# Attention scores of two heads at once, on the upper and lower 64 rows of the array

## Chip, cores and metric

The kernel runs on one core of a Trainium2 chip. The metric is device time in microseconds (us) from start to end of one execution; three runs of the kernel before gave 984.19, 984.31 and 984.76 us, median 984.31 us. The core has five engines that run their own instruction lists in order and meet at semaphores: TensorE (PE, matrix products; PEld is its loading of weights), VectorE (DVE), ScalarE (ACT), GpSimd (POOL) and SyncE (SP), on which this kernel issues all its transfers (DMA).

## The reference, cut to what matters

One decoder layer over 1024 tokens of width 1024: a projection, an attention branch (8 heads), a gated linear branch, their merge, and a gated embedding. The change is in the attention branch:

```python
def mla_attention(q_nope, q_rope, k_nope, k_rope, v):   # 8 heads, 64 + 32 wide; k_rope is shared by all heads
    ...
        sc = (jnp.einsum('bqhd,bkhd->bhqk', qn_i, k_nope).astype(jnp.float32)
              + jnp.einsum('bqhr,bkr->bhqk', qr_i, k_rope).astype(jnp.float32)) * scale
        mask = kpos[None, :] <= qpos[:, None]
        sc = jnp.where(mask[None, None], sc, -jnp.inf)
        pr = jax.nn.softmax(sc, axis=-1).astype(v.dtype)
        return jnp.einsum('bhqk,bkhd->bqhd', pr, v)
```

## The kernel before, in words

**Precision.** Inputs are float32. A factor is split into a rounded high part and the low rest (`split`: ScalarE copies into the rounded type, VectorE subtracts), and a product is the sum of three: high by high, high by low, low by high (`mm3`, lines 145 to 147). A group of such products into one PSUM bank is a `bank`.

**Stages.** First the projections of x and the gated linear branch (0 to some 470 us), then attention (some 548 to 760 us), then the merge, the output product and the gated embedding. Products that have no hurry are interleaved as filler by generators (`stream`, `embed`): in attention these are `yb` (branch output of the linear part, `d<-oh,wh`), later `emb` (`e<-wh,wh`) and the first of `ya` (the attention branch's own output product).

**Attention.** The queries' 32 rope rows of all heads are made in `rope_queries`, four heads at a time, and written to scratch memory (`d_rq`). `make_pair` makes the tiles of two heads: of each head `qh`, `ql`, `kh`, `kl` (high and low part of queries and keys), 96 rows of one tile for the even head (64 plain and 32 rope rows) and 128 for the odd head (its plain rows in the lower half of the tile, its rope rows in the upper half twice, with the key's halved to make up). The product of both heads lands in one bank, so the even head's 64 rows are copied to their own tile by a DMA within SBUF (L864), and rope rows come by DMA from `d_rq` and `krt` (L845, L849, L867, L871). `scores` goes by one head and half of the queries: for each block of 128 queries, over at most 512 keys at a time (a chunk), three products over 96 or 128 rows into a bank `s`; VectorE takes it out with scale, mask and running minimum (L914), ScalarE takes the exponential (L924). `weighted` transposes these rows (`pt`, L963), splits them, and multiplies by the values (`o`, L954 and L955). The loop at the end of the stage interleaves the scores of one head with `weighted` of the one before it, `make_pair` of the next pair, and filler.

**Products over 64 rows elsewhere.** The linear branch has products that use half of the array's rows: L379 (`z`, two rounded products of 512 columns, between full ones) and in `gla` L559, L619, L628 and L690. These float32 products appear as two records each in the trace. In `cross` (L559) the two heads, on rows 0 to 63 and 64 to 127, alternate. At L628 the loop over the two heads is the outer one, so that the eight products of one head stand ahead of the eight of the other:

```python
for hd in range(2):
    for c in range(4):
        for j in (0, 64):
            ...
            nc.tensor.matmul(L[j : j + 32, o0 + 32 : o0 + 64], r32[rows(hd), i0 : i0 + 32], ...)   # shortened
```

**What sets the order.** The order in which code is written is a wish; a scheduler in the compiler sets the order on each engine when the program is built, from its own estimate of times and from when buffers come free. [...] Buffers are `NSLOT` + `NMORE` slots of 4 KB per partition, and the PSUM banks: in attention four `d`, three `s`, one `o`.

## Time and profile before

| | |
|---|---|
| runs | 984.19, 984.31, 984.76 us |
| profiled execution | 983.49 us, span of its instructions 981.7 us |
| TensorE busy | 955.8 us, 97% |
| VectorE, ScalarE, GpSimd busy | 590.2, 413.1, 128.1 us |
| mean granted clock of TensorE | 0.99 |

The span runs from the first to the last instruction; the execution's own time is 1.8 us longer, and 0.8 us below the median of the runs. [...]

### The profile page before, as it was taken

Reading aid. Unit: us, or ns where it says so; the run is one execution under the profiler, and the core shown is the slowest. Engines: PE = TensorE matmul, PEld = TensorE weight load, DVE = VectorE, ACT = ScalarE, POOL = GpSimd, SP = SyncE. Lnnn points to the kernel's source line nnn. Section 1 sums busy time; section 2 is a strip of 40 time slices with the busy share of each in tenths; the row PEclk is TensorE's granted clock in tenths of the full one; section 3 lists DMA queues with packets and bytes.
Section 4 is the critical chain, followed back from the end, with each engine's and each line's share of the span. In section 5 each row is a group of like instructions: output and inputs, shape, how many; then the busy total and the mean of one; then the engine's idle time right before and its main releaser. Section 6 shows DMA issues by size and latency. Waiting matters only on the chain.

```text
span 981.7 us, 14101 instructions
## 1 busy us (share of the span) xinstructions
PE 955.8 (97%) x5216; PEld 794.3 (81%) x5216; DVE 590.2 (60%) x1227; ACT 413.1 (42%) x800; POOL 128.1 (13%) x103
## 2 busy tenths in 40 slices
PE   7999999999999999999999999997999999999995
PEld 5887877887887887888888778886888788889985
DVE  6737765574474474433476469785757863239666
ACT  7306731331331342321333257676885432228333
POOL 2100000000000000001101012235363000000422
PEclk9999999999999999999999999997999999999998
DMA  7200211122222122211253844537146761136112
GB/s 281 94 22 22 65 43 43 57 84 86 76 108 86 63 79 86 97 65 43 82 181 127 230 121 121 133 98 177 49 147 229 254 208 65 49 119 188 53 69 103
DMA packets 47828, 105.70 MB, mean 108 GB/s; under 512 B 6736, under 2 KB 9616, under 8 KB 47760
## 3 DMA queue, kind: packets, MB, share of 16 engines
q1 hardware_dynamic: 47760, 104.81, 33.1%
q8 instruction: 41, 0.67, 0.3%
q14 instruction: 27, 0.22, 0.1%
HBM read 72.18 MB, written 25.20 MB: 99 GB/s over the span
## 4 chain that ended last, share of the span: by engine, by line
PE 86%; DVE 6%; ACT 3%; DMA 3%; issue 2%; SPq 0%; DVEq 0%; ACTq 0%
PE d L145 19%; PE d L147 18%; PE d L146 18%; PE pt L963 3%; PE pg L147 3%; PE pg L146 3%; PE pg L145 3%; PE L L559 2%; PE o L955 2%; PE s L146 2%; PE o L954 2%; PE s L147 2%; PE s L145 2%; PE o L690 1%; DMA kl<-kl 1%
## 5 line engine op out<-in xcount | busy, mean ns | idle before, releaser
L145 PE MATMUL d<-xh,wh 128*128 128x512 f32 x544 | 215.9, 400 | 2.8 <-ACT xh L132 2.6
L146 PE MATMUL d<-xl,wh 128*128 128x512 f32 x544 | 214.5, 395 | 0.1
L147 PE MATMUL d<-xh,wl 128*128 128x512 f32 x544 | 213.3, 393 | 0.1
L145 PEld LDWEIGHTS d<-xh,wh 128*128 128x128 f32 x544 | 103.0, 190 | 28.1 <-ACT xh L132 4.6
L127 ACT ACTIVATE wh<-wr 128x1024 fp32r<-128x1024 f32 (+4 forms) x81 | 76.2, 943 | 114.3 <-DMA wr<-in_w_in 40.4
L146 PEld LDWEIGHTS d<-xl,wh 128*128 128x128 f32 x544 | 103.0, 189 | 21.9 <-DVE xl L133 0.8
L147 PEld LDWEIGHTS d<-xh,wl 128*128 128x128 f32 x544 | 102.7, 189 | 21.9 <-DVE wl L128 0.5
L128 DVE TENSOR_TENSOR wl<-wr,wh 128x1024 fp32r<-128x1024 f32 (+2 forms) x59 | 74.6, 1267 | 71.2 <-ACT wh L127 71.1
L145 PE MATMUL pg<-wh,gh 128*128 128x256 f32 (+1 forms) x200 | 62.7, 314 | 0.0
L146 PE MATMUL pg<-wl,gh 128*128 128x256 f32 (+1 forms) x200 | 62.5, 313 | 0.0
L147 PE MATMUL pg<-wh,gl 128*128 128x256 f32 (+1 forms) x200 | 62.5, 313 | 0.0
L128 DVE TENSOR_TENSOR pt<-pt,pt 128x512 fp32r<-128x512 f32 (+1 forms) x96 | 51.4, 550 | 17.1 <-ACT pt L127 16.9
L494 ACT ACTIVATE z<-z 128x512 f32<-128x512 f32 x32 | 20.2, 631 | 98.0 <-DVE z L466 94.2
L924 ACT ACTIVATE p<-p,nm 128x128 f32<-128x128 f32 (+3 forms) x64 | 49.3, 772 | 21.2 <-DVE nm L914 21.1
L466 DVE TENSOR_TENSOR z<-d,rb 128x512 f32<-128x512 f32 x32 | 22.1, 690 | 51.3 <-PE d L147 51.3
L127 ACT ACTIVATE pt<-pt 128x512 fp32r<-128x512 f32 (+1 forms) x96 | 44.6, 485 | 15.5 <-PE pt L963 13.6
L145 PE MATMUL d<-mh,wh 128*128 128x512 f32 x128 | 50.7, 399 | 0.0
L146 PE MATMUL d<-ol,wh 128*128 128x512 f32 x128 | 50.1, 392 | 0.4 <-DVE ol L128 0.4
L147 PE MATMUL d<-mh,wl 128*128 128x512 f32 x128 | 50.2, 392 | 0.0
L147 PE MATMUL d<-oh,wh 128*128 128x512 f32 x128 | 50.1, 391 | 0.0
L146 PE MATMUL d<-ml,wh 128*128 128x512 f32 x128 | 49.9, 390 | 0.0
L145 PE MATMUL d<-oh,wh 128*128 128x512 f32 x128 | 49.9, 395 | 0.0
(263 smaller groups left out, 1924.4 us busy)
## 6 DMA issues: line engine op xcount, KB each, us to landing
wr<-in_w_in SPq DMA_DIRECT2D x33, 512.0 KB
d_ta<-z SPq DMA_DIRECT2D x16, 256.0 KB
d_tb<-z SPq DMA_DIRECT2D x16, 256.0 KB
tb<-d_tb SPq DMA_DIRECT2D x16, 256.0 KB
d_zb<-tb SPq DMA_DIRECT2D x16, 256.0 KB
d_e<-er SPq DMA_DIRECT2D x16, 256.0 KB
ta<-d_ta SPq DMA_DIRECT2D x16, 256.0 KB
zb<-d_zb SPq DMA_DIRECT2D x16, 256.0 KB
```

The lines of the kernel that those rows point to most:

```text
L127: nc.scalar.activation(dst_hi, src, AF.Copy)
L128: (eng or nc.vector).tensor_tensor(dst_lo, src, f(dst_hi), op=ALU.subtract)
L145: nc.tensor.matmul(ps, lh, rh, start=first, stop=False)
L146: nc.tensor.matmul(ps, lh, rl, start=False, stop=False)
L147: nc.tensor.matmul(ps, ll, rh, start=False, stop=last)
L466: nc.vector.tensor_tensor(z, ps, rb[:, hs(h)], op=ALU.mult)
L494: nc.scalar.activation(z, z, AF.Tanh, scale=0.5)
L559: nc.tensor.matmul(L[:, hd * HALF + c * P : hd * HALF + (c + 1) * P], lt[rows(hd), cs], rt[rows(hd), cs], start=True, stop=True,)
L924: nc.scalar.activation(pt[:, :w], pt[:, :w], AF.Exp, bias=nm, scale=-1.0, accum_out=den)
L954: nc.tensor.matmul(po[:, n0:], vv, ts_[:, n0:HALF], start=kb == 0, stop=False)
L955: nc.tensor.matmul(po[:, n0:], vv, ts_[:, HALF + n0 : S], start=False, stop=kb == nk - 1)
L963: nc.tensor.transpose(pt[:, j * P : (j + 1) * P], pq[j][:, kb * P : (kb + 1) * P], ident)
```

## The change

Both heads of a pair now share tiles: rows 0 to 63 are the even head's, rows 64 to 127 the odd head's, as the product of `make_pair` leaves them in its bank. The rope part is a product of its own. For each chunk a head has five products over 64 rows: `kh,qh`, `kl,qh`, `kh,ql`, and with the rope rows `krt,rh` and `krt,rl`, where `krt` holds high and low part of the shared rope key (32 + 32 rows, and the same again for the lower half), and `rh`, `rl` hold a head's rope queries twice. Each head has its own bank, and the two heads' products are written in turn. `scores` goes by a pair. Both calls of `rope_queries` now stand ahead of the scores, its stores are of two halves, `make_pair` loads `rh` and `rl` by eight DMAs and copies nothing within SBUF. Banks are three `d` and four `s`; there are three more slots, for which the room comes from a smaller `dynamic_dma_scratch_size` (no DMA of this kernel is issued by GpSimd).

```diff
-NMORE = 4
+NMORE = 7
...
-                nc.scalar.activation(krt[64:96], f(krt[0:32]), AF.Copy, scale=0.5)
-                nc.scalar.activation(krt[96:128], f(krt[32:64]), AF.Copy, scale=0.5)
+                nc.scalar.activation(krt[64:128], f(krt[0:64]), AF.Copy)
...
-            get = psum_pool({"d": (HALF, 4), "S": (HALF, 3), "o": (HALF, 1)}, psB)
+            get = psum_pool({"d": (HALF, 3), "S": (HALF, 4), "o": (HALF, 1)}, psB)
...
-                for nm in ("qh", "ql", "kh", "kl"):
-                    for hn in (2 * pr, 2 * pr + 1):
-                        qk[nm, hn] = alloc(F32R, nm)
...
+                for nm in ("qh", "ql", "kh", "kl", "rh", "rl"):
+                    qk[nm, pr] = alloc(F32R, nm)
+                for y, nm in enumerate(("rh", "rl")):
+                    for i in range(4):
+                        r = 32 * (2 * pr % 4 + i // 2)
+                        nc.sync.dma_start(f(qk[nm, pr][32 * i : 32 * i + 32]), d_rq[pr // 2][y][r : r + 32])
...
-                    for y in range(2):
-                        nm = x + "hl"[y]
-                        t0, t1 = f(qk[nm, 2 * pr]), f(qk[nm, 2 * pr + 1])
-                        nc.sync.dma_start(t0[0:64], t1[0:64])
...
-                        mm3(st, qh_[:, qs], ql_[:, qs], kh_[:, c], kl_[:, c], True, True)
...
+                rows = (slice(0, 64), slice(64, 128))
+                q_, k_ = ([qk[n, pr] for n in ns] for ns in (("qh", "qh", "ql", "rh", "rl"), ("kh", "kl", "kh")))
+                k_ += [krt, krt]
...
+                        st = [get("S", "s")[:, :cw] for _ in range(2)]
+                        for i in range(5):
+                            for y, r in enumerate(rows):
+                                nc.tensor.matmul(st[y], q_[i][r, qs], k_[i][r, c], start=i == 0, stop=i == 4)
...
-    nc = bacc.Bacc("TRN2", target_bir_lowering=False, num_devices=1)
+    nc = bacc.Bacc("TRN2", target_bir_lowering=False, num_devices=1, dynamic_dma_scratch_size=1024)
```

The evictions and exponentials are the same in number and size, two heads after each other; the loop around them goes by pair and half, with `weighted` of two heads interleaved.

TensorE before, within the scores of an early head (`s` with its number is one bank; every product reads tiles of 96 or 128 rows, so all of this engine's work there uses the whole array):

```order
L145 MATMUL s_4309<-kh_4161,qh_4157 128x512
L146 MATMUL s_4309<-kl_4163,qh_4157 128x512
L147 MATMUL s_4309<-kh_4161,ql_4159 128x512
L145 MATMUL s_4345<-kh_4161,qh_4157 128x512
L146 MATMUL s_4345<-kl_4163,qh_4157 128x512
L147 MATMUL s_4345<-kh_4161,ql_4159 128x512
```

The two banks are of one head, 512 keys each; its other chunks follow in the same way.

TensorE now, early in the scores (`s_4384` is the even head's bank, `s_4385` the odd head's):

```order
L907 MATMUL s_4384<-kh_4215,qh_4213 128x512
L907 MATMUL s_4385<-kh_4215,qh_4213 128x512
L907 MATMUL s_4384<-kl_4216,qh_4213 128x512
L907 MATMUL s_4385<-kl_4216,qh_4213 128x512
L907 MATMUL s_4384<-kh_4215,ql_4214 128x512
L907 MATMUL s_4385<-kh_4215,ql_4214 128x512
L907 MATMUL s_4384<-krt_620,rh_4217 128x512
L907 MATMUL s_4385<-krt_620,rh_4217 128x512
L907 MATMUL s_4384<-krt_620,rl_4218 128x512
L907 MATMUL s_4385<-krt_620,rl_4218 128x512
L145 MATMUL d_4411<-oh_3282,wh_4329 128x512
```

Here the two heads' products alternate as they are written, and a product over the whole array follows. TensorE now, in the last pair (`s_6345` is the even head's bank, `s_6346` the odd head's; `o` and `pt` use the whole array):

```order
L907 MATMUL s_6345<-krt_620,rh_5701 128x256
L907 MATMUL s_6345<-krt_620,rl_5702 128x256
L954 MATMUL o_6071<-pt_6129,vp 128x512
L953 MATMUL o_6071<-pt_6139,vp 128x512
L962 MATMUL pt_6181<-ident,p_5617 128x128
L962 MATMUL pt_6181<-ident,p_5618 128x128
L954 MATMUL o_6071<-pt_6139,vp 128x512
L962 MATMUL pt_6189<-ident,p_5618 128x128
L953 MATMUL o_6071<-pt_6148,vp 128x384
L907 MATMUL s_6346<-kh_5699,qh_5697 128x256
L907 MATMUL s_6346<-kl_5700,qh_5697 128x256
```

The scheduler has put the five products of one head together and whole-array products between the two heads. Over the stage the 480 products over 64 rows stand in 64 runs, with whole-array instructions between them.

SyncE before, where the tiles of the last pair are filled:

```order
L864 DMA qh_5663<-qh_5664 64x1024
L864 DMA ql_5665<-ql_5666 64x1024
L871 DMA qh_5664<-d_rq_125 16x1024 x4
L871 DMA ql_5666<-d_rq_126 16x1024 x2
L137 DMA wr_5924<-in_pT 128x1024
L871 DMA ql_5666<-d_rq_126 16x1024
L864 DMA kh_5667<-kh_5668 64x1024
L943 DMA d_rc_117<-rr_5831 4x128
L864 DMA kl_5669<-kl_5670 64x1024
```

SyncE now, where the last pair's tiles are filled:

```order
L847 DMA rh_5701<-d_rq_125 32x1024 x2
L942 DMA d_rc_115<-rr_5657 4x128
L137 DMA wr_6008<-in_w_ple 128x1024
L847 DMA rh_5701<-d_rq_125 32x1024 x2
L945 DMA rB_5661<-d_rc_115 64x512
L944 DMA gt_5775<-d_gm_89 64x512
L847 DMA rl_5702<-d_rq_126 32x1024 x4
```

The copies of `qh`, `ql`, `kh` and `kl` within SBUF are gone; the loads of `rh` and `rl` read scratch that was written at the start of the stage. Outside the attention stage and the transfers that prepare it, TensorE's order is the same in both programs (up to its row 1983 of some 4500). On SyncE, ScalarE and VectorE one weight tile of a later product is now loaded and split near the start.

## Rows read from the trace of the kernel before

**Rows 1.** Windows; columns: stretch, length, busy time and count by engine, clock, DMA.

```profile
548.00:600.00 52.00, 49.34 (x272) 41.26 (x272) 35.89 (x103) 28.62 (x68) 8.95 (x7) 1.00 0.57 159
600.00:650.00 50.00, 48.83 (x294) 42.41 (x294) 42.26 (x119) 35.78 (x84) 12.84 (x10) 1.00 0.38 100
650.00:700.00 50.00, 43.81 (x232) 37.73 (x231) 32.77 (x88) 33.22 (x71) 20.22 (x12) 0.86 0.48 131
```

**Rows 2.** Waits of TensorE, 500 to 765 us: total, times, longest.

```profile
PE s L145 <- DVE pt L128: 5.5, 1, 5.5
PE s L146 <- DMA kl<-kl: 1.5, 2, 0.8
PE s L145 <- issue: 0.9, 1, 0.9
PE s L146 <- DMA ql<-d_rq: 0.8, 1, 0.8
```

**Rows 3.** Chain that ended last: start, duration, what.

```profile
673.15 5.92 DMA kl<-kl
```

**Rows 4.** Timeline of TensorE after the wait: start, duration, instruction.

```profile
678.01 0.44 PE L145 MATMUL s<-kh,qh 96*128 96x128 f32 x1 [5.53 <-DVE pt L128]
...
683.34 0.63 PE L147 MATMUL s<-kh,ql 96*128 96x512 f32 x1
683.76 0.63 PE L145 MATMUL s<-kh,qh 96*128 96x512 f32 x1
```

**Rows 5.** Windows around that wait.

```profile
676.00:680.00 4.00, 1.33 (x4) 1.17 (x5) 1.29 (x4) 2.51 (x5) 2.35 (x1) 0.50 0.98 240
...
684.00:688.00 4.00, 4.00 (x18) 3.71 (x18) 2.67 (x11) 2.83 (x10) 2.60 (x2) 0.50 0.32 132
```

**Rows 6.** Timeline of TensorE, score products of 128, 512 and 256 columns.

```profile
553.26 0.27 PE L146 MATMUL s<-kl,qh 96*128 96x128 f32 x1
...
553.37 0.28 PE L147 MATMUL s<-kh,ql 96*128 96x128 f32 x1
...
553.77 0.40 PE L146 MATMUL s<-kl,qh 96*128 96x512 f32 x1
...
554.00 0.40 PE L147 MATMUL s<-kh,ql 96*128 96x512 f32 x1
...
554.35 0.28 PE L146 MATMUL s<-kl,qh 96*128 96x256 f32 x1
...
554.47 0.28 PE L147 MATMUL s<-kh,ql 96*128 96x256 f32 x1
```

**Rows 7.** Groups of TensorE by form, 500 to 765 us: one score product.

```profile
L145 PE MATMUL s<-kh,qh 96*128 96x512 f32 x24 | 10.7, 446 | 0.0
```

**Rows 8.** Timeline of TensorE, two products over 64 rows between products over 128.

```profile
69.61 0.39 PE L147 MATMUL d<-xh,wl 128*128 128x512 f32 x1
69.93 0.73 PE L379 MATMUL z<-glow,wg 64*128 64x512 f32 x2
70.59 0.50 PE L145 MATMUL gv<-wh,xh 128*128 128x512 f32 x1
70.93 0.40 PE L146 MATMUL gv<-wl,xh 128*128 128x512 f32 x1
```

**Rows 9.** Timeline of TensorE, L559: products over 64 rows, two heads in turn.

```profile
128.74 0.39 PE L147 MATMUL d<-xh,wl 128*128 128x512 f32 x1
129.06 1.16 PE L559 MATMUL L<-r 64*128 64x128 f32 x16
130.15 0.50 PE L145 MATMUL d<-xh,wh 128*128 128x512 f32 x1
```

**Rows 10.** Timeline of TensorE, L222: products over all 128 rows.

```profile
459.37 1.84 PE L222 MATMUL ss<-ones,latents 128*128 128x1 f32 x16
```

**Rows 11.** Windows of L628 alone; count is of records running in the stretch.

```profile
142.09:142.25 0.16, 0.15 (x10) 0.16 (x11) 1.00 0.00 0
142.25:142.35 0.10, 0.10 (x22) 0.10 (x20) 1.00 0.00 0
```

## The prediction

> **What bounds the kernel now.** I read the page's busy shares first: TensorE is busy 97% of the span, no other engine above 60%. Most of the program is the same before and after, so I looked only at the attention stage, in windows [rows 1]: TensorE is busy 49.3 of 52, 48.8 of 50 and 43.8 of 50 us, VectorE at most 42.3 of 50. The reader should see that TensorE bounds the stage, with VectorE not far behind, and that the idle time of TensorE there is 2.7 + 1.2 + 6.2 = 10.1 us. The list of waits says what ends that idle time [rows 2]: 5.5 + 1.5 + 0.9 + 0.8 = 8.7 us stand before score products. The 5.5 us are put down to a VectorE instruction, but the chain shows a copy of `kl` within SBUF that lands after 5.92 us just then [rows 3], so the last pair's tiles were late. After that wait the products of 512 columns stand 0.42 us apart (683.34 to 683.76) [rows 4] and the granted clock is 0.50 until some time before 692 [rows 5]; the usual distance is 0.23 us [rows 6]. [...]

> **The products before.** The distance from start to start is the price: 0.11 us for 128 columns, 0.23 for 512, 0.12 for 256 [rows 6]; for 384 I estimate 0.17, which is 0.23 times 384/512. A head has twelve chunks: six of 512, two of 384, two of 256, two of 128 columns (a group of 24 for four heads gives the six [rows 7]). That is 6 x 0.23 + 2 x 0.17 + 2 x 0.12 + 2 x 0.11 = 2.18 us for one product each, and with three products and eight heads 52.3 us.

> **The products now.** A pair has five products per chunk and head, each over half of the rows. If both heads always ran beside each other, they would cost 5 x 4 x 2.18 = 43.6 us; if never, 10 x 4 x 2.18 = 87.2 us. Whether they do can be read from the linear branch. The 16 records of L559, two heads in turn, take 130.15 - 129.06 = 1.09 us with the change of mode below in it [rows 9]; 16 records over all rows, L222, take (1.84 - 0.25) / 15 = 0.106 us each, 1.7 us in all, though they have a single column [rows 10]. So halves of the array do work at the same time, at least in this form. The order of the changed kernel often puts the five products of one head ahead of the five of the other, so it matters whether the second head may start early. L628 has its heads in that order. In its first 0.16 us ten of its records start; in the next 0.10 us 22 are running, of which ten are those, so twelve new ones started in less time [rows 11]. The second head's sixteen therefore began while some of the first head's had not. I take each half as a queue of its own: a run of products costs the longer half's sum. Over the 64 runs in the new order, 23 hold products of one head only and cost 14.8 us, 41 hold both and cost 40.0 us; together 54.8 us, 2.5 us more than before. What the layout could win (8.7 us) the scheduler's grouping takes back.

> **The edges of the runs.** A run over 64 rows stands between products over 128 rows. The row to read is `z`, rounded products over 64 rows with 512 columns, as the new ones are [rows 8]: from the full product before them at 69.61 to the second full product after them at 70.93 there are 1.32 us. Four distances of 0.23 would be 0.92. The other 0.40 us are lost in four places of about 0.1: 0.32 instead of 0.23 from 69.61 to 69.93, another 0.1 within the two `z`, 0.1 before 70.59 and 0.34 instead of 0.23 after it. L559 has the same first step (128.74 to 129.06) [rows 9]. The score products over 96 rows show none of it: they follow each other at their usual distance [rows 6]. [...] At 64 runs the edges cost 64 x 0.40 = 25.6 us. They lie on TensorE, which bounds the stage; nothing hides them unless TensorE waits anyway. Bounds: `z` and L559 both also wait on semaphores at their start, so the edges might cost nothing where no wait stands; the upper bound is the 0.40 of each run.

> **What goes.** No copy within SBUF is left: the pair's product is split into its tile, and `rh` and `rl` come from scratch written long before. The waits on `kl`, `ql` and the first tiles go: -8.7 us. With them goes the stretch at half clock, 678.0 [rows 4] to about 688.1: 10.1 us x (1 - 0.23/0.42) = -4.6 us. What is late next are evictions: VectorE's work is the same, 42 of 50 us in the densest window [rows 1]; there are three `d` banks instead of four for the transposes; and the four `s` banks are only two chunks, since a chunk needs two. For new waits I take +2 us, between 0 and the 8.7 that go, nearer to 0 because a TensorE that has 28 us more work gives the others time to get ahead.

> **What costs nothing.** The two small copies of `krt` become one (ScalarE, 41% busy over the span). `rope_queries` for both groups stands ahead of the scores: the same 18 products, moved. Their eight stores become sixteen, on SyncE, with 36 filler and 30 projection products behind the last of them (66 x 0.23 = 15 us), as against a copy of 5.92 us as the longest seen [rows 3]; if one is later than that, the first `krt,rh` product waits and this falls into the +2. SyncE has 48 fewer transfers. The weight tile loaded early costs a copy each on ScalarE and VectorE at the start, where TensorE has other products to do; I price it at 0, at most 1 us either way.

> **Sum.** +2.5 + 25.6 - 8.7 - 4.6 + 2 = +16.8 us. The profiled execution took 983.5 us, so 1000.3; the runs' median is 0.8 above it, so 1001 us. With the edges at half price it would be 988, and with the larger new waits 1008: the likeliest case's own range is 988 to 1009.

> **Rivals.**
> - *The edges are free (faster).* If TensorE changes between halves and the whole array without loss when no wait stands there, the 25.6 us vanish and the removed waits decide: 1001 - 25.6 = 975 us. For it: each row that shows the loss also has a semaphore wait at its start, and the linear branch's runs are float32, except `z`. Against it: the same 0.09 to 0.11 us in each of the four places, at `z` as at L559, although the waits are on different engines. It decides from the point where a run's edges cost less than (16.8 / 64 =) 0.14 rather than 0.40 us.
> - *Strict order of starts.* If a product never starts before the one ahead of it in the program, the grouped products overlap only where the heads change. Counting the order so, the runs cost 64.6 us instead of 54.8: 1011 us. L628 [rows 11] speaks against it; but it has products of 32 columns, and a queue deep enough for these may not take five of 512 with their weights. [...]
> - *The heads don't run side by side at 512 columns.* No row shows two rounded products of this length in both halves. If they share a path that limits them, the products cost 87.2 us: 1001 + 32.4 = 1033 us. L559 and L628 speak against it, with shorter products.
> - *The tiles stay late.* If `rh` and `rl` wait for slots and land late, the 8.7 and 4.6 us stay: 1014 us. For it: six tiles per pair instead of eight, but two heads' rows `p` at once. Against it: three more slots, and the source is ready early.

> **Chances.** Likeliest case 0.55, free edges 0.19, strict order 0.10, no overlap 0.06, late tiles 0.06, and 0.04 that gains and losses meet within 0.2%, which is about what a measurement of this kernel can tell from no change (2 us). Faster gets nearly all of the free edges, 0.18; same 0.05; slower 0.77. The range reaches from the free edges' 975 to above the late tiles' 1014, 974 to 1016; outside are the case without overlap and the better half of the free edges, together a little under 0.2.

> **What would show it.** In the profile after, score products as 64*128, with a first product of a run about 0.32 us after a full one and 0.34 after the first full one behind it; the sum of score products and edges near 80 us instead of 52; no wait on `kl` and no window at half clock in the stage; the stage some 17 us longer, the stages around it unchanged. Two heads' products that start a few ns apart, also where the order has five of one head first, would show the queues right; 0.23 us between the heads would show strict order. I am wrong if a full product follows a half one after its usual 0.23 us.

## The result, and the profile after

The changed kernel takes 1027.87 us (median of four runs, 1027.56 to 1030.5) against 984.25 (four runs, 982.82 to 984.76): ratio 1.0451, 95% interval 1.0431 to 1.0472. The forecast was 1001 us, 974 to 1016. It is slower, as forecast, but by 43.6 us and not by 16.8. The profiled execution took 1027.97 us, its span is 1026.2; TensorE is busy 989.7 us of it, 96%.

The windows of the attention stage, in the columns of [rows 1]:

```profile
548.00:600.00 52.00, 40.70 (x224) 30.33 (x224) 24.04 (x67) 15.80 (x40) 3.85 (x3) 0.84 0.46 155
600.00:650.00 50.00, 49.31 (x285) 36.51 (x283) 34.48 (x99) 30.02 (x66) 7.73 (x6) 1.00 0.19 54
650.00:700.00 50.00, 48.83 (x290) 36.36 (x289) 34.11 (x92) 31.83 (x70) 12.65 (x9) 1.00 0.23 67
700.00:750.00 50.00, 48.87 (x283) 34.74 (x281) 33.04 (x92) 37.53 (x85) 22.23 (x14) 1.00 0.23 75
```

The hole of before, 43.8 of 50 us at clock 0.86 in the third window, is gone. A new one stands at the start of the stage: 40.7 of 52 us at 0.84. VectorE's densest window has 34.5 of 50 us, before 42.3. The waits of TensorE from 500 to 810 us, against [rows 2]:

```profile
PE s L907 <- DVE ql L128: 11.8, 1, 11.8
PE d L145 <- ACT wh L127: 2.8, 2, 2.2
PE d L145 <- ACT oh L127: 1.6, 1, 1.6
```

Before score products a single wait is left, and none is put down to a copy, as forecast; but that one, of the first score product of all, is 11.8 us. The chain of waits ahead of it, taken from the stretch 515 to 570 us (start, duration, what; [rows 3] was the like):

```profile
529.93 1.74 POOL rt L824
531.69 0.64 ACT rh L127
...
534.10 8.79 DMA d_rq<-rl
542.95 0.30 SPq L847
543.29 0.52 SPq L830
543.86 6.28 DMA d_rq<-rh
550.20 6.21 DMA tb<-d_tb
556.50 1.25 DVE tb L778 x2
...
558.43 1.26 DVE ql L128 x2
559.74 2.67 PE s L907 x15
```

Two stores of the queries' rope to scratch (L830) take 8.79 and 6.28 us from issue to landing, with other stores still on their way before them. SyncE's list has them one behind the other, and in its timeline they start so: the load of `rl` (542.95) reads what the first of them writes and starts when that has landed (534.10 + 8.79 = 542.89); the next stores of the second group start behind that load (543.29), and the loads of `tb` (for the filler) behind these (550.20). The loads of `tb` also need a temporary tile. `rt`, `rh`, `rl` and `tb` share six of them (`t2`), and before loads of `tb` SyncE waits 1.8 and 2.0 us more for the landings of two stores from these tiles. VectorE waits 8.9 us for the first `tb`, works on it and two more from 556.50, and starts the split of `ql`, which the first score product needs, only behind that (558.40). So that split, which reads nothing of what is stored, is held by two engines' queues and by the temporary tiles. The clock around it (windows; [rows 5]):

```profile
555.00:559.00 4.00, 0.00 (x0) 0.00 (x0) 2.50 (x5) 0.00 (x0) 0.00 (x0) 0.50 0.54 197
559.00:563.00 4.00, 3.71 (x22) 3.13 (x23) 3.42 (x12) 0.88 (x4) 0.00 (x0) 0.50 0.58 202
563.00:567.00 4.00, 4.00 (x12) 3.09 (x11) 0.33 (x2) 1.10 (x4) 0.00 (x0) 0.53 0.86 295
567.00:571.00 4.00, 4.00 (x23) 3.00 (x22) 1.73 (x5) 1.31 (x4) 0.00 (x0) 1.00 0.20 73
```

The stretch at half clock has moved with the wait: after it TensorE works for some 7 us at a granted clock of 0.50, its products of 512 columns 0.42 us apart (563.36 to 563.78). A second, short one (785.2 to 788.6) follows the wait of 2.2 us on `wh`:

```profile
785.00:789.00 4.00, 4.00 (x14) 3.24 (x13) 4.00 (x10) 2.44 (x5) 2.57 (x2) 0.57 0.70 198
```

Now the products themselves, TensorE's timeline where nothing waits ([rows 6, 8]; x2 are the two heads):

```profile
575.35 0.39 PE L147 MATMUL d<-oh,wh 128*128 128x512 f32 x1
575.67 0.50 PE L907 MATMUL s<-kh,qh 64*128 64x512 f32 x2
576.00 0.40 PE L907 MATMUL s<-kl,qh 64*128 64x512 f32 x2
576.24 0.40 PE L907 MATMUL s<-kh,ql 64*128 64x512 f32 x2
576.47 0.40 PE L907 MATMUL s<-krt,rh 64*128 64x512 f32 x2
```

Both heads go in one distance: 576.00 to 576.47 is 0.235 us for a pair, the 0.23 of one full product before. The first step costs 0.32 instead of 0.23, as at `z`, and the second 0.33, and the view shows no idle time there. Where the order has five products of one head first ([rows 11] was the like):

```profile
578.50 0.49 PE L907 MATMUL s<-kh,qh 64*128 64x512 f32 x1
578.83 0.39 PE L907 MATMUL s<-kl,qh 64*128 64x512 f32 x1
578.84 0.50 PE L907 MATMUL s<-kh,qh 64*128 64x512 f32 x1
579.06 0.39 PE L907 MATMUL s<-kh,ql 64*128 64x512 f32 x1
579.18 0.40 PE L907 MATMUL s<-kl,qh 64*128 64x512 f32 x1
```

The order has all five of the first head before the second's. The second's `kh,qh` starts at 578.84, ahead of the first's third, fourth and fifth. From there both halves run beside each other. So in these rows TensorE ran its list in order within each half alone.

Where TensorE's time went. I summed its records of the stage, each from its start to the next one's start, since their durations overlap (0.40 us at a distance of 0.235 above), idle time apart (before 470 to 765 us, after 470 to 810):

| us | before | after | difference | forecast |
|---|---|---|---|---|
| score products `s` | 59.0 | 70.7 | +11.7 | |
| `o` | 38.9 | 45.7 | +6.8 | |
| `pt` | 26.6 | 34.4 | +7.8 | |
| these three: products and edges | 124.5 | 150.7 | +26.3 | +28.1 |
| idle | 10.0 | 19.7 | +9.7 | -6.7 |
| filler and projections `d<-oh`, `d<-ol` (290 and 296 products) | 67.3 | 74.0 | +6.8 | |
| half clock, within the rows above (estimate) | 4.3 | 4.9 | +0.6 | -4.6 |

The edges also fall on what stands next to a run (behind `z` the first full product costs 0.34 us instead of 0.23 [rows 8]), so `o` and `pt` grow too. The last row is TensorE's time at clock 0.5 (9.4 us before, 10.8 after) times the prediction's 1 - 0.23/0.42. Before, it lies in `s`, `o` and `pt` almost alone (9.2 us); after, 3.8 us lie there and 7.1 in `d`. So at full clock the three would differ by an estimated 26.3 + 4.2 - 1.7 = +28.8 us. Of the +6.8 of `d`, six products more in the stretch are 1.4 and the half clock 3.2. The differences +26.3, +9.7 and +6.8 make 42.8 of the span's 44.5 us.

### The profile page after: what moved, and what is told of

It is laid out like the page before. It is cut to its first block, busy times and chain, and to the rows that moved or that the text cites. A ratio compares the mean times of both kernels' runs of the same rounds, so it can differ in the third digit from the quotient of the medians.

```text
span 1026.2 us, 14397 instructions
## 1 busy us (share of the span) xinstructions
PE 989.7 (96%) x5408; PEld 797.5 (78%) x5408; DVE 592.1 (58%) x1227; ACT 414.3 (40%) x799; POOL 131.3 (13%) x103
## 3 DMA queue, kind: packets, MB, share of 16 engines
q1 hardware_dynamic: 45264, 98.51, 28.8%
## 4 chain that ended last, share of the span: by engine, by line
PE 84%; DMA 7%; DVE 4%; ACT 1%; issue 1%; POOL 1%; SPq 1%; DVEq 0%; ACTq 0%; POOLq 0%
PE d L145 17%; PE d L147 17%; PE d L146 17%; PE s L907 7%; PE pg L147 3%; PE pg L146 3%; PE pg L145 3%; PE pt L962 3%; PE L L558 2%; PE o L954 2%; PE o L953 2%; DMA tb<-d_tb 1%; PE gv L146 1%; PE gv L145 1%; PE gv L147 1%
## 5 line engine op out<-in xcount | busy, mean ns | idle before, releaser
L128 DVE TENSOR_TENSOR wl<-wr,wh 128x1024 fp32r<-128x1024 f32 (+2 forms) x59 | 72.5, 1231 | 69.9 <-ACT wh L127 69.8
L923 ACT ACTIVATE p<-p,nm 128x128 f32<-128x128 f32 (+7 forms) x64 | 49.4, 772 | 45.9 <-DVE nm L910 45.5
L145 PE MATMUL d<-oh,wh 128*128 128x512 f32 x128 | 52.1, 411 | 4.3 <-ACT wh L127 2.2
L127 ACT ACTIVATE pt<-pt 128x512 fp32r<-128x512 f32 (+1 forms) x96 | 44.4, 484 | 25.4 <-PE pt L962 24.8
L147 PE MATMUL d<-oh,wh 128*128 128x512 f32 x128 | 51.9, 405 | 0.2 <-DVE wh L128 0.2
L465 DVE TENSOR_TENSOR z<-d,rb 128x512 f32<-128x512 f32 x32 | 22.1, 690 | 49.3 <-PE d L147 49.3
```

Of the source, the lines that this page charges most:

```text
L127: nc.scalar.activation(dst_hi, src, AF.Copy)
L128: (eng or nc.vector).tensor_tensor(dst_lo, src, f(dst_hi), op=ALU.subtract)
L145: nc.tensor.matmul(ps, lh, rh, start=first, stop=False)
L147: nc.tensor.matmul(ps, ll, rh, start=False, stop=last)
L465: nc.vector.tensor_tensor(z, ps, rb[:, hs(h)], op=ALU.mult)
L923: nc.scalar.activation(pt, pt, AF.Exp, bias=nm[y], scale=-1.0, accum_out=den4[y][:, qb - 4 * hf : qb - 4 * hf + 1])
```

## Experiments

Ratios are to the kernel before on the same chip (in brackets the 95% interval); 1% is 9.8 us. Five of them (3, 4, 5, 7 and 13) leave work out, as their expectations say. Idle times of TensorE are from 470 to 810 us of each span (before: 10.4, the change: 19.7).

| kernel | median us | ratio |
|---|---|---|
| changed kernel | 1027.87 | 1.0451 (1.0431 to 1.0472) |
| 1 rope stored whole | 1020.30 | 1.0331 (1.0282 to 1.0380) |
| 2 products of a chunk held together | 1128.01 | 1.1449 (1.1372 to 1.1525) |
| 3 pairs, whole array | 1012.60 | 1.0250 (1.0176 to 1.0324) |
| 4 before, middle product over 64 rows | 1024.83 | 1.0374 (1.0295 to 1.0453) |
| 5 as 3, four `d` banks | 992.87 | 1.0069 (1.0049 to 1.0089) |
| 6 as 1, late rope | 1025.58 | 1.0384 (1.0355 to 1.0413) |
| 7 before, no copies | 975.37 | 0.9875 (0.9847 to 0.9902) |
| 8 as 1, heads in turn | 1017.32 | 1.0303 (1.0269 to 1.0337) |
| 9 as 1, four `d` banks | 1020.24 | 1.0351 (1.0327 to 1.0375) |
| 10 before, three `d` banks | 1009.24 | 1.0234 (1.0199 to 1.0268) |
| 11 before, copies earlier | 987.28 | 1.0019 (0.9996 to 1.0042) |
| 12 before, rope first | 992.13 | 1.0080 (1.0052 to 1.0107) |
| 13 as 5, late rope | 984.27 | 0.9983 (0.9960 to 1.0006) |
| 14 as 9, late rope | 1021.83 | 1.0366 (1.0335 to 1.0397) |

**1. Rope stored whole.** The changed kernel with the stores of before.

```diff
-d_ = d_rq[g][y].rearrange("(h s r) c -> s h r c", s=2, h=4)
-for s_ in range(2):
-    nc.sync.dma_start(d_[s_][:, :, hs(h)], f(r_[64 * s_ : 64 * s_ + 64]))
+nc.sync.dma_start(d_rq[g][y][:, hs(h)], f(r_))      # and rh, rl read back 16 rows at a time
```

> The changed kernel with one edit: the rope queries are stored as in the kernel before (one transfer of 128 rows per part and half instead of two of 4 x 16 rows), and read back by 16 rows. Theory: the new transfers of 4 x 16 rows land late (6 to 9 us in the chain), hold SyncE's list and the temporary buffers, and so cause the wait of 11.8 us ahead of the first score product and some 3.7 us at half clock behind it; without them 1028 - 15 = about 1012 us. Rival: the start of the stage is late because both rope groups stand ahead of the scores and because of three d banks, whatever the form of the store; then the wait stays and the time is 1024 to 1028 us.

1.2% less than the change, in the middle between the two. The edit also reads `rh` and `rl` back in 64 loads instead of 32. The wait before the first score product, and a store in the chain:

```profile
PE s L906 <- DVE ql L128: 2.8, 2, 2.6
```

```profile
531.80 2.18 DMA d_rq<-rh
```

2.18 us for a whole tile of 256 KB, where halves of 128 KB took 6.28 and 8.79; the longest wait falls from 11.8 to 2.6 us, so most of it came from the form of the store. With the stores under way, the busy share of the 16 DMA engines (the last column but one) was 0.26 in the change, as much as 4.2 engines busy throughout, and 0.98 in 1; what in the pattern makes the difference is not shown:

```profile
534.00:539.80 5.80, 5.80 (x27) 4.80 (x26) 1.75 (x3) 0.00 (x0) 1.19 (x1) 1.00 0.26 97
```

```profile
532.80:534.00 1.20, 1.20 (x7) 1.00 (x6) 1.17 (x3) 0.00 (x0) 0.00 (x0) 1.00 0.98 362
```

Some 33 us over the kernel before remain.

**2. A chunk's ten products held together** (the kernel of 1, with a critical section around them).

```diff
+with tc.tile_critical():
     for i in range(5): ...
```

> The kernel of e1_store_whole, and the ten score products of a chunk kept together and in their written order (48 runs over 64 rows instead of 65; by halves as queues the products cost 43.6 us instead of 55.3). Theory: each run costs about 0.4 us at its edges, so 17 x 0.4 + 11.7 = 18 us less than e1, about 993 us. Rival: ten products that need two free banks at once make TensorE wait for evictions, which takes the gain back: within 5 us of e1.

It failed as an experiment: the section also stops what stands around it, TensorE is idle 75.5 us, much of the stage runs at half clock (its mean from 500 to 750 us is 0.84), and the two longest of many waits are these:

```profile
PE s L907 <- ACT p L923: 16.6, 12, 2.3
PE s L907 <- issue: 9.1, 9, 3.6
```

**3. Whole array** (the kernel of 1, three products a head over all 128 rows; no edges).

```diff
-for i in range(5):
-    for y, r in enumerate(rows):
-        nc.tensor.matmul(st[y], q_[i][r, qs], k_[i][r, c], start=i == 0, stop=i == 4)
+for y in range(2):
+    mm3(st[y], q_[0][:, qs], q_[2][:, qs], k_[0][:, c], k_[1][:, c], True, True)
```

> The kernel of e1_store_whole, but each head's scores are three products over all 128 rows of the shared tiles instead of five over 64 (the scores then mix two heads, and the rope part is left out). Layout, transfers, banks and loop stay. Theory: the slowdown that is left in e1 is score products and run edges alone: 55.3 + 65 x 0.4 - 52.3 = 29 us less than e1, about 983 us, and up to 10 us less if a run costs more than 0.4. Rival: the loop by pairs and the banks cost the time; then it stays within 8 us of e1.

Only 7.7 us less than 1, so the rival, it seemed. But TensorE was idle 27.8 us where 1 is idle 12.8: with the edges gone something else held it. What, 5 tells.

**4. The kernel before with edges.** Each chunk's middle product over 64 rows, 96 runs of one product with no wait between.

```diff
-mm3(st, qh_[:, qs], ql_[:, qs], kh_[:, c], kl_[:, c], True, True)
+nc.tensor.matmul(st, qh_[:, qs], kh_[:, c], start=True, stop=False)
+nc.tensor.matmul(st, qh_[0:64, qs], kl_[0:64, c], start=False, stop=False)
+nc.tensor.matmul(st, ql_[:, qs], kh_[:, c], start=False, stop=True)
```

> The kernel before with the second of the three score products of a chunk over 64 rows instead of 96 or 128 (its other rows are left out of that product). Nothing else changes: 96 runs of one product, each between two whole-array products of the same bank with no wait between them. Theory: a run costs 0.40 us at its edges also where no semaphore wait stands: 984 + 96 x 0.40 = 1022 us. Rival: the loss in the linear branch's rows came from their waits, and a change of halves is free: 984 us.

1.0374 is +37 us: the edges are not free. TensorE's timeline, a chunk of 512 and one of 128 columns:

```profile
611.47 0.40 PE L912 MATMUL s<-kh,qh 96*128 96x512 f32 x1
611.80 0.50 PE L913 MATMUL s<-kl,qh 64*128 64x512 f32 x1
612.23 0.50 PE L914 MATMUL s<-kh,ql 96*128 96x512 f32 x1
612.57 0.40 PE L912 MATMUL s<-kh,qh 96*128 96x512 f32 x1
...
613.66 0.22 PE L912 MATMUL s<-kh,qh 96*128 96x128 f32 x1
613.81 0.33 PE L913 MATMUL s<-kl,qh 64*128 64x128 f32 x1
614.07 0.33 PE L914 MATMUL s<-kh,ql 96*128 96x128 f32 x1
614.23 0.28 PE L941 MATMUL rcT<-ident,rc 128*4 128x128 f32 x1
```

Neither of these two middle products, nor the one after each, has a semaphore to wait for. From chunk to chunk 1.10 us (611.47 to 612.57) instead of 3 x 0.23: 0.41 more. With 128 columns 0.57 instead of 0.33: 0.24. Part of the 37 us is half clock: TensorE works 38 us of the stage at 0.5 (551 to 568 and 705 to 729 us), before 9.4. With that taken out (the estimate of above), `s`, `o` and `pt` cost 33 us more by their records, 0.35 a run.

**5. Four `d` and three `s` banks**, on the kernel of 3.

```diff
-{"d": (HALF, 3), "S": (HALF, 4), "o": (HALF, 1)}
+{"d": (HALF, 4), "S": (HALF, 3), "o": (HALF, 1)}
```

> The kernel of e3_whole_array (three products per head over all rows, scores of two heads mixed, rope part left out) with four d banks and three s banks as in the kernel before, instead of three and four. e3 has no run edges and no more products than the kernel before, and is still some 25 us slower, with 30 us of idle TensorE. Theory: three d banks are too few for the transposes of two heads, whose evictions then hold TensorE up; with four the time falls to 990 to 1000 us. Rival: the loop by pairs leaves TensorE short of filler where VectorE and ScalarE have two heads' evictions at once; the banks don't matter, 1008 to 1015 us.

18 us less (within 8, the intervals being wide for 3): the idle time falls from 27.8 to 17.9 us. So three `d` banks were part of the floor that 3 had run into; which of its waits hang on them is not shown. **10** puts the change's banks into the kernel before (the edit the other way round):

> The kernel before with three d banks and four s banks, nothing else changed. Theory (the fourth d bank is worth 18 us wherever score products stand one head at a time): about 1000 us, ratio 1.015 or more, idle time of TensorE between 500 and 765 us well over the 10 us of before. Rival (the price belongs to the order of the loop by pairs, in which the two heads' score tiles come in couples, and not to the banks alone): 980 to 988, ratio under 1.005.

As the theory had it and more, +2.3%, idle 25.0 us against 10.4. Its longest waits:

```profile
PE s L145 <- DVE pt L128: 9.3, 2, 6.9
PE o L955 <- DVE pt L128: 3.9, 7, 1.3
PE s L145 <- DVE nm L914: 3.4, 1, 3.4
```

So I took the banks for the missing term, and **9** gave them back to the kernel of 1 (the same edit):

> The kernel by pairs with the rope stored whole (1020, ratio 1.033), and with four d banks and three s banks as before instead of three and four. Theory (three d banks hold the products of the next pair and of the output back also beside the edges): about 18 us less, as with the whole array, so near 1002 (ratio 1.015). Rival (with pairs two s banks are taken at once, so the fourth s bank is worth at least what the fourth d bank is): within 6 us of 1020, either side, and the idle time of TensorE between 500 and 850 us stays at 14 us or more.

The rival: 1.0351 against 1.0331, no gain. Against the rival's second half the idle time does fall, from 12.8 to 9.2 us, but `s` rises from 71.8 to 80.9: counted in TensorE's order there are 70 runs that cost 63.3 us by the prediction's way of counting, against 65 and 55.3, and 33 of them hold one head only, against 25. That with three `s` banks the second head often finds no bank is the likely reason, not shown by itself. For this loop the two cannot be told apart within the intervals.

**6. Late rope**: the kernel of 1, the second `rope_queries` in the loop as before.

```diff
-for g in range(2):
-    for _ in rope_queries(g): pass
+for _ in rope_queries(0): pass
+late_rope = rope_queries(1)          # advanced at blocks (1, 1) and (2, 3) of the loop
```

> The kernel of e1_store_whole with the second rope group back inside the loop over the scores, as in the kernel before (and one more slot, which its tables need). Theory: what is left of the wait at the start of the stage in e1 (2.8 us at the first score product, 3 us more idle before it) comes from the second rope group's place: 1020 - 6 = 1014 us, no wait over 1 us there. Rival: the start has no part in what is left; 1018 to 1022 us.

No gain, on the rival's side: the 0.5% above 1 lies within the intervals. The wait at the start is gone, others take its place, and the idle time is 19.3 us instead of 12.8. **12** is the other side, the kernel before with both groups first (the same edit backwards):

> The kernel before with the rope of the second group of heads formed ahead of the loop, as the change has it, and not within it; tiles, copies and loop otherwise as before. Theory (DVE's splits for the first pair then stand behind sixteen more evictions, and TensorE waits 5 to 6 us at the start of the heads, as in the kernels by pairs): a wait on DVE's ql of 4 to 8 us between 530 and 575 us in the waits, and 4 to 8 us more in all, ratio 1.004 to 1.008. Rival (the work only moves, and what it leaves in the loop runs without the wait of 5.5 us on DVE there): ratio within 0.3% of 1, whatever the start waits.

The time is as the theory had it, +0.8%, the place only in part: 2.7 us at the start, and larger waits than before at the copies for the pairs, which I had not expected:

```profile
PE s L145 <- DMA kl<-kl: 5.2, 1, 5.2
PE d L145 <- DVE ql L128: 2.7, 1, 2.7
...
PE s L145 <- DMA kh<-kh: 2.0, 2, 1.5
```

**7. The kernel before without copies** (both heads read the odd head's tile).

```diff
-qk[nm, hn] = alloc(F32R, nm)         # and no copies at L845, L849, L864 to L871
+qk[nm, 2 * pr] = qk[nm, 2 * pr + 1] = alloc(F32R, nm)
```

> The kernel before, with both heads of a pair reading the odd head's tile, and without the copies and rope loads that fill the tiles (the scores mix two heads and leave out the rope part; all score products have 128 rows). Everything else stays: the loop by heads, four d and three s banks. Theory: the waits of 8.7 us and the 4.6 us at half clock behind them hang on these transfers alone: 984 - 13 = 971 us. Rival: other waits take their place, 980 us or more.

-1.25%: the waits and the half clock that the prediction let go (13.3 us) are worth 12.3 where the transfers are left out. **11** tries to have them with the whole reference kept, by advancing `make_pair` two steps with each block:

> The kernel before, in which the preparation of the next pair advances two steps instead of one with each query block, so that the fills of its tiles (kh<-kh, kl<-kl and the rope rows) are issued sooner; nothing is left out. Theory (the waits on these copies and on DVE at the pair's start are 8.7 us that a kernel by one head can avoid by timing alone): 975 to 980, ratio 0.991 to 0.996. Rival (SP's queue, not the step at which the copies are written, sets when they start, or the products moved forward now wait on evictions): 982 to 990.

The rival: no gain. The wait of 5.5 us is gone, others (the longest before `o`, 2.6 us) make an idle time of 12.6 us instead of 10.4, and by the mean granted clock, 0.989 against 0.990, a stretch of some 14 us at half clock is there as before. Of the versions tried that compute the whole, none beats the kernel before.

**8. Heads in turn**: the kernel of 1, the ten products of a chunk tied to their written order.

```diff
+tc.add_manual_dep(now.ins, last.ins.name, NoSync, reason="heads in turn")   # shortened
```

> The kernel of e1_store_whole with the ten products of a chunk held to the order in which they are written (two heads in turn); other instructions may still stand between them. There are 67 runs instead of 65, and by halves as queues the products cost 46.9 us instead of 55.3. Theory: 8.4 us less, and 0.8 us more for edges: 1020 - 7.6 = 1013 us. Rival: TensorE waits for evictions instead, since in e3 it idled when its products were short; within 3 us of e1.

`s` falls by 8.5 us (71.8 to 63.3), 67 runs whose products cost 46.9 us, and the time by 3, which is the rival (the intervals, some 0.5%, don't tell it from nothing). Idle time takes 4.5 us back (17.3), half clock some 2, `o` and `pt` 1.5.

**13 and 14. The loop by pairs alone.** 13 is 5 with late rope, 14 is 9 with late rope (edits as in 6).

> The loop by pairs with three products a head over the whole array (its scores mix the heads and leave the rope out), four d and three s banks, and the second rope group formed within the loop as in the kernel before. Theory (the 19 us between the same products in a loop by heads, 975.4, and in the loop by pairs, 992.9, are some 8 us of rope formed first and some 11 us of the loop by pairs itself): 983 to 988, ratio 0.997 to 1.003. Rival A (the rope first is all of it): 974 to 978, ratio under 0.993. Rival B (moving the rope gives nothing here, as it gave nothing with half-array products): 990 or more, ratio 1.005 or more.

> The kernel by pairs with all that stands beside the products undone: rope stored whole, second rope group within the loop, four d and three s banks. Theory (the half-array products and their edges cost 28 us on whatever loop they stand in): 28 us above the same loop with whole-array products, so 1011 to 1016 if that takes 983 to 988, ratio 1.026 to 1.032. Rival (the edges hide part of the other waits, so that the sum is not additive): under 20 us or over 35 us above it.

13 confirms its theory: 0.9983, 8.5 us under 5. 14 falls on the rival's side: 1.0366, 38 us above 13 (within 4), not 28. One window, 500 to 750 us, of 14 and then of 13:

```profile
500.00:750.00 250.00, 250.00 (x1302) 186.57 (x1301) 161.91 (x400) 131.63 (x291) 55.90 (x40) 1.00 0.30 94
```

```profile
500.00:750.00 250.00, 242.89 (x1290) 204.25 (x1289) 178.92 (x434) 153.16 (x344) 76.48 (x55) 0.99 0.40 122
```

In this window TensorE of 14 has no idle time at all and the full clock (in the whole stage it is idle 5.5 us), and the kernel is still 36 us slower than before. That is the plainest proof that half-array products cost TensorE time of its own. Its order has 81 runs at 67.7 us by the prediction's counting; why the scheduler mixes more here is not shown.

## Why the prediction was wrong

**The products and their edges: right**, in kind and size (an edge is what the prediction also calls the change of mode). Forecast +28.1 us; by the records of the change itself +26.3, and +28.8 at full clock. Two heads go in the time of one (0.235 us a pair), and one half does not wait for the other (578.84 against 579.06); what the prediction inferred from how fast records of L628 start, the rows at 578.50 to 579.52 show directly. What is left for an edge after the counted products is (28.8 - 2.5) / 64 = 0.41 us in the change; likewise, from `s`, `o` and `pt` against the whole-array kernel on the same loop, (35.8 - 11.0) / 70 = 0.35 in 9 and (39.6 - 15.4) / 81 = 0.30 in 14. The 0.40 read at `z` was a good value, at the upper end; short columns cost less (0.24 at 128).

That 9 takes 27.8 us longer than 5 (2.82%, within 0.31), from which it differs in these products alone, looks like the forecast's 28.1 and is luck: with 9's 70 runs the prediction's way gives 11.0 + 28.0 = 39.0. The records show 35.8, and the time rises less because the idle time falls from 17.9 to 9.2 us.

**The waits that go: right** for the work, by 7: -12.3 us for the -13.3 of the forecast. One reading in it was loose: the copy of `kl` [rows 3] lands at 679.07, and the 5.5 us had ended at 678.01 [rows 4]. It ended the next wait, of 0.66 us. With all copies and rope loads left out (7), the 5.5 us are gone all the same.

**New waits, +2 us: the step that failed**, with its neighbour "What costs nothing". In the change's trace the stage is idle 19.7 us and not 10.0 - 8.7 + 2 = 3.3. So the new waits are 18.4 us where the forecast had 2 and at most 8.7, and 11.8 of them are the one wait ahead of the first score product, which falls to 2.6 with the stores of before (1). Half clock, forecast at -4.6, came out at +0.6, with stretches at 0.50 beside the new waits of 11.8 and 2.2 us. These two terms are 16.4 + 5.2 = 21.6 of the 26.8 us by which the forecast fell short.

The experiments show where such time comes from. One way from the kernel before to the change, each step the difference of two measured ratios (x 984 us):

| step | kernels | us |
|---|---|---|
| no copies | before, 7 | -12.3 |
| loop by pairs, whole array | 7, 13 | +10.6 |
| rope first | 13, 5 | +8.5 |
| half-array products and edges | 5, 9 | +27.8 |
| banks three and four | 9, 1 | -2.0 |
| rope stored in halves | 1, change | +11.8 |

They sum to 44.4. The forecast had -13.3, +28.1 and +2. On this way the +2 became 10.6 + 8.5 - 2.0 + 11.8 = 28.9 us. Intervals are some 0.3 to 0.55% (3 to 5 us) for a step, so the -2.0 is not told from nothing. That the step of the stores is 11.8 us, as the wait is, is chance: the wait fell by 9.2.

The sizes hang on the order of the steps. By 13, 14 and 9 instead of 13, 5 and 9, the half-array products are +37.7 us and the rope's place -1.5. 14 is idle 3.7 us less than 9, but with 81 runs instead of 70 its products and edges cost 4.7 more; in 6, against 1, the idle time even grows. So the stores are shown as a cause (1). The rope's place costs 8 to 9 us in the loops over the whole array (12, with waits at the copies that the change doesn't have, and 5 against 13), and on the loop with half-array products nothing. The 10.6 of the loop by pairs is measured, but which part of it (two heads' tiles at once, the rope loads that 13 has and 7 has not, the later start of `make_pair`, the order of `weighted`) stays open.

The two sentences that misled: "a TensorE that has 28 us more work gives the others time to get ahead" holds within the loop, where no score product waits any more, and not at its start, where nothing is ahead yet. And the sixteen stores were priced by the products that stand behind them and by the longest copy seen, 5.92 us, when what mattered was the form of their pattern, the temporary tiles that they hold, and the two queues behind them: SyncE's (`tb`) and VectorE's (`tb`, then `ql`). The prediction expected a late store to hold the first `krt,rh` product, which reads it; it held `ql`, which doesn't.

**The rivals.** Free edges: refuted by 4 and 14. Strict order, and no overlap: refuted by the timelines of the change (578.84 before 579.06; a pair in 0.235 us). Tiles that stay late: the nearest in kind, a late start with half clock after it, but at the start of the stage and through the stores, which that rival didn't name; and its 1014 us were too low.

## What to carry to other kernels

Count the changes between parts of the array before you put two small products side by side: here each run cost 0.30 to 0.41 us beyond its products, more than a full product of 512 columns (0.23), and more than all that working side by side could win. Price a changed DMA by its access pattern (here 97 GB/s in the one and 362 in the other), by the buffers that it holds and by what stands behind it on the issuing and the receiving engine's queue, not by when its data is needed. And an experiment that removes one limit can show the next one instead (3 looked like cheap edges until the banks were put back), so undo a second suspect before you read its small difference. And where steps hide each other's waits, sizes read one after the other hang on the order: check them against idle time and records of the trace itself.
